# Sorting products of the dilated heads: exact bf16 parts and a bf16 0/1 matrix in place of float32

## The chip, the cores and the metric

One core of a Trainium2 chip runs the whole program. The time is the device time of one execution in microseconds (us); the figure for a kernel is the median of its runs. Engines are named as in the profile: PE (TensorE matmuls), PEld (TensorE weight loads, which lie beside the matmuls), DVE (VectorE), ACT (ScalarE), POOL (GpSimd), SP (the queue that issues most transfers). L547 is line 547 of the kernel before.

## The reference

The reference is one encoder block on a 1024 x 1024 float32 input: RMSNorm, a combined q/k/v projection, two groups of attention heads (4 differential heads, 8 dilated heads), an output projection with a residual, then RMSNorm, a router, 16 expert-choice SwiGLU experts and a last RMSNorm. What matters here is the mix of patterns in the dilated heads. Each pattern gives an output and the logarithm of its softmax denominator, and the patterns are mixed by a softmax over those logarithms:

```python
lse = jax.nn.logsumexp(s, axis=-1)
p = jnp.exp(s - lse[..., None])
o = jnp.einsum('brhnqk,brhnkd->brhnqd', p.astype(v.dtype), vn)
...
w = jax.nn.softmax(jnp.stack(lses, axis=0), axis=0)
o = jnp.sum(w[..., None] * jnp.stack(outs, axis=0).astype(jnp.float32), axis=0)
```

The kernel does not form the logarithms. For each query it keeps a (negated) maximum and a sum of exponentials per branch, and computes the mixing weights from these.

## The kernel before

**Stages.** Up to about 55 us: the first norm, its transposes and the first projection block. From there to about 400 us the eight dilated heads run, two heads to a unit, four units, with the twelve projection blocks poured in between as filler for PE. From about 390 us to 640 us the four differential heads run, then the output projection, the second norm, the router and the ranking, and from about 740 us on the experts, whose weights stream from memory through a ring of tiles.

**One dilated unit.** It is cut into 8 groups (two heads by four parts `j`). For each group there are four steps: `scores` (eight matmuls into the tile `ps`, L154 through the helper `mm`; the biased maximum on DVE, L416; the exponential and its sum on ACT, L418), `turn` (eight transposes into two `pt` tiles, L157 through the helper `tp`, with copies on ACT and DVE), `mix` (ten matmuls into `av`) and `gather` (L537, L538). The loop over the groups runs these as a pipeline: at step n it emits `scores(n)`, filler, one late step of the unit before if there is one, `turn(n-1)`, filler, `mix(n-2)`, `gather(n-2)`, filler.

**The two statistics tiles.** The near branch keeps its maxima and sums in `stN`, in natural order of the queries. The other branch works on queries sorted by their position modulo 4, so its maxima and sums, in `stM`, are in that order: each is a tile of 128 partitions by 32 float32 (two heads, maximum and sum, eight tiles of queries). Both get the maximum from DVE (L416) and the sum from ACT (L418).

**The late steps.** After the last `gather` of a unit four late steps are queued, one of them emitted in each later group, and for the fourth unit all at once: `regroup`, then `weights` and `spread`, then `combine(0)` and `combine(1)`. `regroup` (L541 to L551) brings `stM` into natural order by multiplying with 0/1 matrices, which are 128-column cuts of the tile `sort`: 16 float32 calls of 8 columns, which the profile shows as 32 matmuls and 32 weight loads, into a `pt` tile of the pool `ps_t` (two buffers, shared with the transposes), and one DVE copy to `sM`:

```python
for c in range(4):
    for r in range(4):
        x = 128 * c - r + 3
        nc.tensor.matmul(pm[:, :, c], sort[:, x:x + 128],
                         U["stM"].rearrange("p i s (r a) -> p r a i s", r=4)[:, r],
```

`weights` (L557 to L567) forms the mixing weights on DVE and ACT, `spread` (L574) widens them on POOL into `wr`, `combine` transposes `wr` on PE, mixes on DVE (L586 to L589), splits the result (L96) and stores it to `o_d` through SP (L592). The matrix `sort` is made once: an iota on POOL (L734) and a compare on DVE (L735).

**What sets the order.** PE, DVE, ACT, POOL and SP each run their instructions in a fixed order. That order is made when the program is built, by a scheduler that goes by program order, by what is ready and by its own estimate of durations: an instruction that is ready early may be put on an idle engine far ahead of its place in the program.

**What follows the dilated heads.** `open_left` frees their tiles, and the loads of the first differential head (L617, L618 for q and k, L621 for the bias, L627 for v) are issued on SP, some of them behind the stores of the last unit (L592).

Of the kernel before, what the change touches and what calls it, by code (L numbers as in the profile page):

```python
# [10 lines left out]
F32 = mybir.dt.float32  # L11
F32R = mybir.dt.float32r
BF = mybir.dt.bfloat16
I32 = mybir.dt.int32
AF = mybir.ActivationFunctionType
OP = mybir.AluOpType
# [3 lines left out]
S = 1024  # L20
D = 1024
NT = S // 128
# [60 lines left out]
def tile_hybrid_encoder_block(ctx, tc, x, norm1_g, w_in, lam_v, subln_g, w_out, rel_bias, hot,  # L83
                              norm2_g, w_router, w_moe, norm_f_g, steps, out, n_experts=E, dbg=None):
    nc = tc.nc
# [108 lines left out]
    ps_t = st_p.enter_context(tc.tile_pool(name="ps_t", bufs=2, space=PS))  # L194
# [231 lines left out]
    def dilated_unit(u):  # L426


        U = {}
# [110 lines left out]

        def regroup():  # L541

            pm = ps_t.tile([128, 2, 4, 2, 2], F32, name="pt")
            for c in range(4):
                for r in range(4):
                    x = 128 * c - r + 3
                    nc.tensor.matmul(pm[:, :, c], sort[:, x:x + 128],  # L547
                                     U["stM"].rearrange("p i s (r a) -> p r a i s", r=4)[:, r],
                                     start=(r == 0), stop=(r == 3))
            U["sM"] = sm_a.tile([128, 2, 2, NT], F32, name="sM")  # L550
            nc.vector.tensor_copy(U["sM"].rearrange("p i s (a c) -> p a c i s", a=2), pm)  # L551

        def weights():
            stN, sM = U["stN"], U["sM"]
# [22 lines left out]
        def combine(n):  # L577
# [3 lines left out]
            for k in range(2):  # L581
                pr = ps_t.tile([128, 4, 128], F32, name="pt")
                for t in range(4):
# [11 lines left out]
                   lambda i=i, j=j: gather(i, j)) for i in range(2) for j in range(4)]  # L595
        loads = [lambda i=i, h=h: load(i, h) for i in range(2) for h in range(2)]
        return loads, groups, [regroup, lambda: (weights(), spread(0), spread(1)), lambda: combine(0), lambda: combine(1)]

    def dense_unit(u):
# [114 lines left out]
    PA = {}  # L714
    fill = projections()

    def run(gen, n):
        for _ in range(n):
            next(gen, None)
# [10 lines left out]
            nc.gpsimd.memset(r32(tl), 0.0)  # L730
        PA["pair"].append(pr)

    sort = PA["dw"].tile([128, 516], F32, name="sort", bufs=1)
    nc.gpsimd.iota(sort.bitcast(I32), pattern=[[1, 516]], base=-3, channel_multiplier=-4)  # L734
    nc.vector.tensor_scalar(sort, sort.bitcast(I32), 0.0, None, op0=OP.is_equal)  # L735
    run(fill, FILL1)

    loads, groups = [], []
# [200 lines left out]
    with st_w as st:  # L939
# [4 lines left out]
        ps_t = st.enter_context(tc.tile_pool(name="ps_t3", bufs=2, space=PS))  # L944
# [290 lines left out]
    rem = rt.tile([128, NT, E], F32, name="tok")  # L1235
# [337 lines left out]
```

## Time and profile before

| what | value |
|---|---|
| median of 3 runs | 2278.7 us (2278.2 to 2278.9) |
| the profiled execution | 2276.6 us, its span 2274.8 us |
| PE busy | 2180.2 us, 96% of the span |
| DVE busy | 1891.9 us, 83% |
| ACT busy | 1601.4 us, 70% |
| POOL busy | 218.3 us, 10% |
| mean granted clock of PE | 0.981 |
| chain that ended last | PE 86%, DVE 5%, DMA 4%, issue 2%, ACT 2% |

The profile is of one execution. Its span runs from the first to the last instruction; the execution's time has about 1.8 us more, which lies around the span. Busy times overlap between engines, so what a change in one stage is worth is read from that stage: from its timeline, from what each engine waited for there, and from the chain of waits that ended last. In the windows view the clock is that which was granted to TensorE, as a share of full speed.

### The profile page before, as it was taken

Reading aid. Unit: us, or ns where it says so; the run is one execution under the profiler, and the core shown is the slowest. Engines: PE = TensorE matmul, PEld = TensorE weight load, DVE = VectorE, ACT = ScalarE, POOL = GpSimd, SP = SyncE. Lnnn points to the kernel's source line nnn. Section 1 sums busy time; section 2 is a strip of 40 time slices with the busy share of each in tenths; the row PEclk is TensorE's granted clock in tenths of the full one; section 3 lists DMA queues with packets and bytes.
Section 4 is the critical chain, followed back from the end, with each engine's and each line's share of the span. In section 5 each row is a group of like instructions: output and inputs, shape, how many; then the busy total and the mean of one; then the engine's idle time right before and its main releaser. Section 6 shows DMA issues by size and latency. Waiting matters only on the chain.

```text
span 2274.8 us, 31909 instructions
## 1 busy us (share of the span) xinstructions
PE 2180.2 (96%) x11115; PEld 1619.0 (71%) x11235; DVE 1891.9 (83%) x2870; ACT 1601.4 (70%) x2431; POOL 218.3 (10%) x244
## 2 busy tenths in 40 slices
PE   8999999889996999999999999999999999999995
PEld 7899989667874566666766766676676676666663
DVE  6466674567777999999899999999999999999996
ACT  5576773456753567777787777787777777877785
POOL 1000100245533000000000000000000000000000
PEclk9999999999997999999999999999999999999997
DMA  5866555579568899999999999999999999999983
GB/s 182 236 177 196 173 156 154 167 189 246 183 195 284 278 352 391 368 391 388 375 390 373 387 381 373 404 373 383 383 378 401 365 384 390 374 387 380 387 347 130
DMA packets 172750, 708.26 MB, mean 311 GB/s; under 512 B 19690, under 2 KB 54634, under 8 KB 106658
## 3 DMA queue, kind: packets, MB, share of 16 engines
q1 hardware_dynamic: 160452, 670.46, 79.8%
q0 software_dynamic: 7184, 25.69, 3.9%
q10 hardware_dynamic: 4952, 10.05, 1.2%
q8 instruction: 89, 1.46, 0.3%
q14 instruction: 73, 0.60, 0.1%
HBM read 649.89 MB, written 57.75 MB: 311 GB/s over the span
## 4 chain that ended last, share of the span: by engine, by line
PE 86%; DVE 5%; DMA 4%; issue 2%; ACT 2%; POOL 0%; SPq 0%; ACTq 0%; POOLq 0%; DVEq 0%
PE pg L1343 14%; PE pg L1344 14%; PE pg L1352 13%; PE pm L154 10%; PE py L1385 7%; PE py L1384 7%; PE py L1381 6%; PE av L154 4%; PE pt L157 3%; PE ps L154 3%; PE py L154 2%; PE px L1364 2%; DVE wl L1315 1%; DMA w<-in_w_moe_dram 1%; PE pt L547 1%
## 5 line engine op out<-in xcount | busy, mean ns | idle before, releaser
L1315 DVE TENSOR_TENSOR wl<-w,wh 128x1024 bf16<-128x1024 f32 (+1 forms) x1062 | 1236.3, 1213 | 75.4 <-ACT wh L1313 72.0
L1313 ACT ACTIVATE wh<-w 128x1024 fp32r<-128x1024 f32 (+1 forms) x1070 | 1041.6, 1041 | 8.6 <-DMA h_d<-xp 5.7
L1343 PE MATMUL pg<-wh,xh 128*128 128x512 f32 x1408 | 569.2, 404 | 0.0
L1344 PE MATMUL pg<-wh,xl 128*128 128x512 f32 x1408 | 552.4, 392 | 1.4 <-DVE xl L96 1.4
L1352 PE MATMUL pg<-wl,xh 128*128 128x512 bf16 x1313 | 316.5, 380 | 6.3
L1384 PE MATMUL py<-wh,eh 128*128 128x512 f32 x704 | 310.7, 441 | 0.0
L1343 PEld LDWEIGHTS pg<-wh,xh 128*128 128x128 f32 x1408 | 264.7, 188 | 56.3 <-issue 2.0
L1344 PEld LDWEIGHTS pg<-wh,xl 128*128 128x128 f32 x1408 | 265.1, 188 | 53.8 <-DVE xl L96 2.2
L1385 PE MATMUL py<-wh,el 128*128 128x512 f32 x704 | 278.3, 395 | 0.0
L1352 PEld LDWEIGHTS <-xh 128*128 128x128 bf16 x1408 | 123.6, 98 | 170.0 <-issue 45.1
L1370 ACT ACTIVATE eh<-px 128x256 fp32r<-128x256 f32 x176 | 67.6, 384 | 166.1 <-PE px L1364 166.1
L1381 PE MATMUL py<-wl,eh 128*128 128x512 bf16 x701 | 180.4, 379 | 1.0 <-ACT eh L1370 0.9
L1384 PEld LDWEIGHTS py<-wh,eh 128*128 128x128 f32 x704 | 132.4, 188 | 44.3
L1357 ACT ACTIVATE sg<-pg 128x256 f32<-128x256 f32 x176 | 67.5, 384 | 135.6 <-PE pg L1352 135.6
L1385 PEld LDWEIGHTS py<-wh,el 128*128 128x128 f32 x704 | 132.5, 188 | 28.7 <-issue 0.4
L154 PE MATMUL pm<-hT,wh 128*128 128x512 f32 x464 | 147.7, 399 | 0.1
L1381 PEld LDWEIGHTS <-eh 128*128 128x128 bf16 x704 | 68.8, 98 | 80.4 <-ACT eh L1370 1.2
L1444 POOL DMA_INDIRECT x_d<-row,idx x15 | 24.1, 1607 | 933.8 <-ACT row L1443 933.8
L154 PE MATMUL pm<-wh,hT 128*128 128x256 f32 x512 | 102.6, 291 | 0.4 <-ACT hT L96 0.2
L154 PEld LDWEIGHTS pm<-hT,wh 128*128 128x128 f32 x464 | 85.0, 190 | 16.0 <-DVE ee L361 0.5
L96 DVE TENSOR_TENSOR pl<-pt,ph 128x512 fp32r<-128x512 f32 x96 | 65.2, 683 | 36.2 <-ACT ph L96 36.2
L418 ACT ACTIVATE e<-e,nm 128x1024 f32<-128x1024 f32 x64 | 73.4, 1147 | 27.5 <-DVE nm L416 21.1
(299 smaller groups left out, 2907.4 us busy)
## 6 DMA issues: line engine op xcount, KB each, us to landing
w<-in_w_moe_dram SPq DMA_DIRECT2D x514, 1024.0 KB, 7.3
w<-in_w_moe_dram SPq DMA_DIRECT2D x56, 256.0 KB, 4.3
wraw<-in_w_in_dram SPq DMA_DIRECT2D x48, 256.0 KB, 3.7
v_d<-ee SPq DMA_DIRECT2D x16, 512.0 KB, 3.7
q_d<-ee SPq DMA_DIRECT2D x16, 512.0 KB, 3.7
k_d<-ee SPq DMA_DIRECT2D x16, 512.0 KB, 3.5
k<-k_d SPq DMA_DIRECT2D x16, 512.0 KB, 6.5
xt<-in_x_dram SPq DMA_DIRECT2D x8, 512.0 KB, 6.8
```

Source lines behind the costliest of these rows:

```text
L154: return pin(nc.tensor.matmul(*args, **kw))
L157: return pin(nc.tensor.transpose(*args, **kw))
L418: nc.scalar.activation(e, e, AF.Exp, bias=nm, scale=-1.0, accum_out=l)
L1313: hi = nc.scalar.activation(wh[:, cs], src, AF.Copy)
L1315: sub = eng.tensor_sub(wl[:, cs], src, r32(wh)[:, cs])
L1343: hh = nc.tensor.matmul(pg, xh[:, k, :], wh, start=(k == 0), stop=False)
L1344: mm_ = nc.tensor.matmul(pg, xl[:, k, :], wh, start=False, stop=False)
L1352: low = nc.tensor.matmul(pg, top(xh)[:, k, :], cut(k)[1], start=False, stop=(k == KD - 1))
L1370: in_turn(nc.scalar.activation(eh, pt, AF.Copy))
L1381: low.append(lambda j=j, c=c, ns=ns, n=n: nc.tensor.matmul(py[:, ns], top(eh)[:, j, :], wl(c, 512), start=(s == 0 and j == 0), stop=False))
L1384: nc.tensor.matmul(py[:, ns], eh[:, j, :], wh(c, 512), start=False, stop=False),
L1385: nc.tensor.matmul(py[:, ns], el[:, j, :], wh(c, 512), start=False, stop=(s == NS - 1 and j == 1))))
```

## The change

The matrix `sort` becomes bf16. `regroup` first cuts `stM` into three bf16 parts whose sum is the float32 value (24 bits in three times 8), with five instructions on POOL: a copy to bf16, a subtraction, a copy, a subtraction, a copy. The 16 calls then multiply bf16 by bf16 with 24 columns each instead of 8, into a `pt` tile three times as large, and two DVE reductions add the three parts, in place of the one copy. The integer scratch for making `sort` is taken from a tile of the pool `er`, since `sort` itself is too narrow now.

```diff
         def regroup():
-            pm = ps_t.tile([128, 2, 4, 2, 2], F32, name="pt")
+            st, rem = U["stM"], PA["dw"].tile([128, 2, 2, NT], F32, name="rem", bufs=1)
+            parts = PA["dw"].tile([128, 2, 2, NT, 3], BF, name="parts", bufs=1)
+            for n in range(3):
+                nc.gpsimd.tensor_copy(parts[:, :, :, :, n], st)
+                if n < 2:
+                    nc.gpsimd.tensor_sub(rem, st, parts[:, :, :, :, n])
+                    st = rem
+            pm = ps_t.tile([128, 2, 4, 2, 2, 3], F32, name="pt")
             for c in range(4):
                 for r in range(4):
                     x = 128 * c - r + 3
                     nc.tensor.matmul(pm[:, :, c], sort[:, x:x + 128],
-                                     U["stM"].rearrange("p i s (r a) -> p r a i s", r=4)[:, r],
+                                     parts.rearrange("p i s (r a) n -> p r a i s n", r=4)[:, r],
                                      start=(r == 0), stop=(r == 3))
             U["sM"] = sm_a.tile([128, 2, 2, NT], F32, name="sM")
-            nc.vector.tensor_copy(U["sM"].rearrange("p i s (a c) -> p a c i s", a=2), pm)
+            for i in range(2):
+                nc.vector.tensor_reduce(U["sM"][:, i].rearrange("p s (a c) -> p a c s", a=2), pm[:, :, :, i],
+                                        axis=mybir.AxisListType.X, op=OP.add)
...
-    sort = PA["dw"].tile([128, 516], F32, name="sort", bufs=1)
-    nc.gpsimd.iota(sort.bitcast(I32), pattern=[[1, 516]], base=-3, channel_multiplier=-4)
-    nc.vector.tensor_scalar(sort, sort.bitcast(I32), 0.0, None, op0=OP.is_equal)
+    sort = PA["dw"].tile([128, 516], BF, name="sort", bufs=1)
+    places = PA["er"].tile([128, S], F32, name="ed").bitcast(I32)[:, 0:516]
+    nc.gpsimd.iota(places, pattern=[[1, 516]], base=-3, channel_multiplier=-4)
+    nc.vector.tensor_scalar(sort, places, 0.0, None, op0=OP.is_equal)
```

## Rows read from the trace of the kernel before

**Rows 1.** Windows view: busy us (count) of each engine, PEclk, DMA share, GB/s.

```profile
90.00:400.00 310.00, 307.96 (x2100) 282.55 (x2098) 193.91 (x557) 200.24 (x497) 18.69 (x57) 0.99 0.62 174
860.00:2100.00 1240.00, 1234.66 (x5694) 859.09 (x5773) 1141.24 (x1251) 968.08 (x1223) 38.21 (x27) 1.00 0.98 383
```

**Rows 2.** Chain that ended last, 60 to 420 us: start, us, what.

```profile
164.10 3.47 PE pt L547 x32
...
236.82 3.67 PE pt L547 x32
...
304.29 3.47 PE pt L547 x32
...
370.54 3.47 PE pt L547 x32
...
388.47 10.90 DMA w<-q_d
```

**Rows 3.** Timeline, first regroup: start, us, engine, what, [idle before <-releaser].

```profile
163.93 3.63 PE L547 MATMUL pt<-stM,sort 128*128 128x8 f32 x32
...
167.42 0.63 PE L157 MATMUL pt<-ident,ed 128*128 128x128 f32 x4
...
167.60 0.21 DVE L551 COPY sM<-pt 128x32 f32<-128x32 f32 x1 [1.55 <-PE pt L547]
```

**Rows 4.** Timeline, PE at 810 us: 16-column bf16 products, then 112 to 16 columns.

```profile
810.86 0.36 PE L1193 MATMUL px<-gt,ones_b 128*128 128x16 bf16 x8 [1.30 <-DVE gt L1190]
...
811.18 0.38 PE L1182 MATMUL pr<-eq,ones_b 128*128 128x112 bf16 x7
```

**Rows 5.** One line's view, L1193: ns min/median/max, first and last start.

```profile
L1193 PEld LDWEIGHTS <-ones_b x8: 95/96/99, 810.9 to 811.0; 128*128 128x128 bf16 x8
```

**Rows 6.** Windows view around the second and fourth regroup, columns as in Rows 1.

```profile
236.70:240.40 3.70, 3.70 (x35) 3.66 (x33) 1.88 (x3) 2.43 (x4) 0.00 (x0) 1.00 0.55 164
240.40:243.40 3.00, 3.00 (x17) 3.00 (x17) 1.16 (x3) 1.86 (x3) 0.00 (x0) 0.58 0.77 291
243.40:247.00 3.60, 3.60 (x29) 3.60 (x28) 2.81 (x12) 3.49 (x11) 0.16 (x1) 0.88 0.09 35
...
307.60:311.00 3.40, 3.40 (x21) 2.91 (x21) 2.02 (x7) 1.31 (x3) 0.16 (x1) 1.00 0.02 5
...
374.00:377.40 3.40, 3.40 (x10) 2.62 (x10) 1.60 (x10) 0.23 (x1) 1.25 (x3) 0.50 1.05 223
```

**Rows 7.** Timeline after the second regroup, ACT and the PE weight loads.

```profile
241.54 0.60 ACT L512 ACTIVATE pair<-pt 128x512 fp32r<-128x512 f32 x1 [2.36 <-PE pt L157]
...
254.77 0.19 PEld L154 LDWEIGHTS pm<-hT,wl 128*128 128x128 f32 x1 [0.45 <-DVE wl L334]
```

**Rows 8.** Tile view of stM: ns min/median/max, first and last start.

```profile
L418 ACT ACTIVATION_READ_ACCUMULATOR ed<-ed,stM x64: 185/188/202, 91.1 to 353.8; 128x1 f32 x64
```

**Rows 9.** Timeline of POOL: start, us, what, [idle before <-releaser].

```profile
1.18 0.12 POOL L952 MEMSET rank<- 128x40 f32 x1
...
16.02 0.45 POOL L292 TENSOR_TENSOR rl<-rb,rh 34x128 fp32r<-34x128 f32 x1
...
141.01 0.21 POOL L447 MEMSET k<- 128x128 f32 x1 [7.18 <-PE ps L154]
...
376.15 2.28 POOL L574 COPY wr<-ea 128x512 f32<-128x512 f32 x4 [32.67 <-DVE ea L567]
```

**Rows 10.** Tile view of wr: ns min/median/max, first and last start.

```profile
L574 POOL COPY wr<-ea x16: 604/613/3033, 175.4 to 377.8; 128x512 f32<-128x512 f32 x16
```

**Rows 11.** Timeline at 2096 us, a DVE reduction from PSUM.

```profile
2096.45 0.16 DVE L1223 TENSOR_REDUCE num<-pr 128x1 f32<-128x2 f32 x1 [1.74 <-PE pr L1221]
```

**Rows 12.** Timeline, way from the last unit to the differential heads.

```profile
383.87 2.50 SPq L592 DMA_DIRECT2D o_d<-wr  x2
...
386.42 0.56 SPq L621 DMA_DIRECT2D w<-ta_d  x1
...
397.88 1.09 PE L154 MATMUL ps<-w 128*128 128x512 f32 x4
...
402.15 2.04 PE L154 MATMUL ps<-w 128*128 128x512 f32 x4 [3.18 <-issue]
```

## The prediction

> **What bounds the kernel now.** I read the windows first, then the chain of waits, then the timeline around the four regroups. From 90 to 400 us PE is busy for 308 of 310 us, while DVE and ACT are at 63% and 65% and POOL at 6% [rows 1]: in the stage of the change PE is the bound, and there is always a projection block to fill it. The chain that ended last agrees: all four regroups stand on it, with 3.47, 3.67, 3.47 and 3.47 us, together 14.08 us [rows 2]. The timeline shows why it is so much. A regroup writes only 8 columns per product, yet its 32 float32 products hold PE from 163.93 until the next transposes at 167.42 us, 3.49 us or 109 ns each [rows 3]. The time goes into weights that are loaded anew for each product.
>
> What comes later doesn't undo a shift. The experts' stage has PE busy for 99.6% and the DMA engines at 98% [rows 1], and whichever of the two sets its pace, it starts when the stages ahead of it let it: its loads hang on tiles that these free, not on the clock on the wall. So a microsecond taken from PE before 370 us should be a microsecond at the end.
>
> **The change part by part.** *The products.* 32 float32 products per unit become 16 of bf16, each in one pass, with 24 columns. The nearest rows are eight bf16 products of 16 columns, each with its own load: 0.36 us for all eight, where one alone takes 0.17 [rows 4, 5], so they follow each other at (0.36 - 0.17) / 7 = 27 ns. Seven of 112 down to 16 columns take 0.38 us [rows 4], 35 ns apart, so that 24 columns instead of 16 cost next to nothing. At 31 ns, 16 products are 0.5 us. Per unit 14.08 / 4 - 0.5 = 3.0 us is saved, and 12.1 us over four. The bounds are 27 ns (0.43 us, 12.4 us saved) and the 109 ns of today's products (1.74 us, 7.1 us saved); I take the bf16 rows, since they have type and shape of the new ones. One thing differs: half of the cuts of the matrix start at an odd bf16 column.
>
> A load of 128 columns is one place where the notes speak against the change: the Trainium skill, "TensorE: Matmul & The Clock Gate", section "LDWEIGHTS (loading the stationary operand)", gives a load as its columns over 1.2 GHz whatever they hold, 107 ns here, and 16 in a row would then be 1.7 us (an estimate from that page). The row shows loads of 95 to 99 ns each, of which eight start within about 0.2 us [rows 5], so they overlap. I go by the row, and keep the other as a rival.
>
> *The clock.* After the second and the fourth regroup the granted clock fell: 0.58 from 240.4 to 243.4 us and 0.88 until 247.0, and 0.50 from 374.0 to 377.4; after the third it stayed at 1.00 [rows 6]. What PE did before it fell was over 3.5 us of 8-column products at full clock [rows 6]. Lost were 0.42 x 3.0 + 0.12 x 3.6 = 1.7 us and 0.5 x 3.4 = 1.7 us of PE's time. With 0.5 us of products I expect neither fall, but I count nothing for it. In unit 2 ACT is the next in line: it stood idle for 2.36 us until the transposes behind the regroup came, and at 254.77 us PE was already waiting for weights that ACT and DVE had to cut [rows 7]. If ACT sets the pace, this unit gains 2.4 us, if PE does, 3.1 + 1.7 = 4.8; I take 3.1, nearer to ACT's row. In unit 4 PE has too little work anyway: it finishes its scores at about 399 us and starts the next at 402.15, after a load that took 10.90 us [rows 2, 12]. PE work done faster there only lengthens that wait.
>
> *The fourth unit's own path.* The loads that PE waits for at 402 us stand on SP behind the two stores of the last unit [rows 12], and these behind weights, spread and combine. All of that starts where the regroup ends, so the 3.0 us of this unit count through this path. It gets two reductions for the one copy of 0.21 us [rows 3]. The nearest reduction took 0.16 us on 2 elements [rows 11]; between 0.16 and 0.3 us each I take 0.2, hence 0.2 us more. In units 1 to 3 the later maxima wait for nothing but combine, whose PE work is filler; nothing.
>
> *The split on POOL.* Five instructions on 32 elements each: the rows bound one by 0.12 us (a memset of 40 elements) and 0.45 us (a subtraction of 128) [rows 9], at worst by 3.03 us, the longest of the 512-element copies, whose median is 0.61 [rows 10]. I take 0.25 each, 1.3 us per unit. I cost it at nothing, because it is covered: unit 1 ends its scores at 141.0 us, when POOL's memset of a key tile is released [rows 9], and some 4 us later its sums are there; the regroup comes at 163.9 [rows 3]. In unit 4 the last sum is written at 354.0 [rows 8], the regroup starts 16 us later, and POOL is idle for 32.67 us until 376.15 [rows 9]. That the scheduler uses such room is to be seen from a memset of the ranking, which ran at 1.18 us [rows 9], hundreds of microseconds ahead of its place. What is queued on POOL behind the split (memsets of keys, values and scores) has several microseconds of slack each. If this cover is gone, PE's queue waits for the split with all that stands behind it; that is a rival. Making the matrix keeps its iota and its compare, now from a borrowed buffer that is free then: nothing.
>
> **The sum.** 12.1 - 0.2 = 11.9 us less. The profiled execution took 2276.6 us and would take 2264.7; the median of the runs is 2.1 us above it, and 2278.7 - 11.9 = 2266.8 us.
>
> **The rivals.** *Loads one after the other.* If the weight loads of the odd cuts, or all, don't overlap, 16 x 98 ns [rows 5] are 1.6 us per unit, and (3.5 - 1.6) x 4 - 0.2 = 7.4 us are saved: 2271.3 us. For it: today's products stand at 109 ns. Against it: the bf16 rows.
>
> *The gain is taken in by the next wait.* ACT in unit 2 and the loads at 402 us show such waits already. If DMA throughput and not the end of the stores sets the landing at 399 us (the DMA share was 1.05 from 374.0 to 377.4 [rows 6]), all that the four units gain meets the same landing, and if the same holds for the experts' weights at a share of 0.98 [rows 1], between 0 and 4 us are left, 2276.7 us in the middle. Against it: every one of these transfers is issued by something that moves forward too.
>
> *PE waits for the split (slower).* The place is PE's queue at the first product of each unit. If the scheduler leaves the split beside the regroup, the whole of it stands on the path; it costs as much as is saved at five instructions of 0.6 us, the median of the 512-element copies. At 0.8 us it is 4.0 - 3.0 = 1.0 us per unit lost, 4 us in all, and PE standing still would lower the clock in units 1 and 3 as well, 2 x 1.7 us: 2286.1 us. The Trainium skill, "GPSIMD Engine Reference", section "Engine selection", sends elementwise work to VectorE, as GpSimd is about twice as slow with two inputs; that matters only if the split is uncovered, and no row here shows these five. Against this rival: 19 and 16 us of cover.
>
> **How the numbers follow.** The forecast has 0.67, loads one after the other 0.10, the gain taken in 0.11, PE waiting for the split 0.07; 0.05 is for an order that the scheduler makes anew with other waits, split evenly over the three results. Single steps at this length are uncertain by one fall of the clock, 1.7 us, either way. The forecast's own range is 2263 (12.4 - 0.2 and both falls of 1.7 us won) to 2270; taking in the rival of the loads and one more fall of the clock, and 2 us below for a luckier order, the range is 2261 to 2273. A measurement of this kernel can tell about 0.2%, 4.6 us, from no change. Forecast and loads give faster, with a third of the rest, 0.79; the gain taken in gives the same time, 0.12; the split on the path slower, 0.09.
>
> **What would show it.** The 16 products within 0.6 us per unit, at about 30 ns; the five POOL instructions ending microseconds before; no idle of PE that ends with them; the granted clock at 1.00 after all four; the dense scores of 402.15 us at about 390. It is wrong if the products stand at 100 ns, if PE waits for POOL ahead of the first of them, or if the dense scores come 12 us sooner and the end doesn't.

## The result and the profile after

The change made the kernel faster by 0.5%, little but clear of the noise: 2268.2 us median (2264.1 to 2271.0, six runs) against 2279.9 us (2278.2 to 2285.0, six runs) on the same chip, a ratio of 0.995 with a 95% interval of 0.9936 to 0.9964, 11.6 us. The forecast was 2266.8 us, 11.9 less. The profiled execution took 2268.57 us, span 2266.8, clock 0.981 as before; its partner took 2276.63, faster than any of the six runs of before. So the two traces differ by 8.1 us only, and 8.1 is what they can explain. PE's busy time over the span fell by 12.0 us, from 2180.2 to 2168.2.

The timeline of PE after the change; columns as in [rows 3]:

```profile
163.90 0.57 PE L555 MATMUL pt<-parts,sort 128*128 128x24 bf16 x16
164.32 0.42 PE L157 MATMUL pt<-ident,ed 128*128 128x128 f32 x2
...
233.60 0.57 PE L555 MATMUL pt<-parts,sort 128*128 128x24 bf16 x16
234.02 0.36 PE L154 MATMUL pm<-wh,hT 128*128 128x256 f32 x1
...
235.61 0.50 PE L154 MATMUL ps<-kc,qc 128*128 128x256 f32 x2 [0.55 <-ACT kc L422]
...
247.88 0.50 PE L154 MATMUL pm<-hT,wl 128*128 128x512 f32 x1 [0.40 <-DVE wl L334]
...
298.12 0.56 PE L555 MATMUL pt<-parts,sort 128*128 128x24 bf16 x16
...
361.27 0.57 PE L555 MATMUL pt<-parts,sort 128*128 128x24 bf16 x16
361.69 0.48 PE L154 MATMUL pm<-hT,wh 128*128 128x512 f32 x1
```

Sixteen products hold PE from 163.90 to 164.32, 0.42 us or 26 ns each, where 32 held it for 3.49 [rows 3]; the other units give 0.42, 0.41 and 0.42. No idle time stands in brackets at any of the four, so PE waited for nothing there. It does wait behind the second, for ACT's `kc` at 235.61 and for DVE's `wl` at 247.88: work that PE used to cover [rows 7] now ends last. The view of line L555 (ns min/median/max, first and last start):

```profile
L555 PEld LDWEIGHTS <-sort x64: 95/97/101, 163.9 to 361.6; 128*128 128x128 bf16 x64
L555 PE MATMUL pt<-parts,sort x64: 176/181/191, 163.9 to 361.7; 128*128 128x24 bf16 x64
```

A load takes 97 ns (96 in [rows 5]), and a product 181, but they start 26 ns apart: they overlap, odd cuts and even ones alike. In before a load of the float32 kind took 192 ns, and these pairs followed each other at 109 ns:

```profile
L547 PEld LDWEIGHTS pt<-stM,sort x128: 186/192/193, 163.8 to 373.7; 128*128 128x128 f32 x128
```

Why a float32 pair takes four times the spacing of a bf16 pair, no run separates. The timeline of POOL shows the split, three of its five instructions in the first unit and two in the fourth:

```profile
144.82 0.24 POOL L547 CAST parts<-stM 128x32 bf16<-128x32 f32 x1 [2.52 <-ACT ed L418]
145.15 0.25 POOL L549 TENSOR_TENSOR rem<-stM,parts 128x32 f32<-128x32 f32 x1
...
146.09 0.24 POOL L547 CAST parts<-rem 128x32 bf16<-128x32 f32 x1
...
344.98 0.24 POOL L547 CAST parts<-stM 128x32 bf16<-128x32 f32 x1 [10.61 <-ACT ed L418]
...
346.25 0.24 POOL L547 CAST parts<-rem 128x32 bf16<-128x32 f32 x1
```

The split runs from 144.82 to 146.33, 1.5 us, and is done 17.6 us before PE needs it; in the fourth unit 14.8 us before. The view of the tile `sM` has the two reductions (0.20 us each):

```profile
L560 DVE TENSOR_REDUCE sM<-pt x8: 199/203/209, 165.9 to 362.0; 128x16 f32<-128x48 f32 x8
```

The windows of the stage and of the 3.4 us from each regroup on, with the columns of [rows 1]:

```profile
90.00:400.00 310.00, 300.83 (x2053) 271.19 (x2052) 199.11 (x573) 203.58 (x505) 23.94 (x78) 0.98 0.64 181
...
163.60:167.00 3.40, 3.40 (x36) 2.90 (x36) 3.09 (x16) 3.12 (x9) 0.00 (x0) 1.00 0.96 279
233.40:236.80 3.40, 2.85 (x36) 2.48 (x35) 2.32 (x6) 3.35 (x6) 0.00 (x0) 1.00 0.50 137
298.00:301.40 3.40, 3.40 (x36) 2.95 (x35) 2.35 (x14) 3.09 (x10) 0.16 (x1) 1.00 0.49 178
361.00:364.40 3.40, 3.40 (x30) 2.58 (x29) 1.71 (x11) 0.23 (x1) 0.31 (x1) 1.00 1.05 328
```

The clock stays at 1.00 behind all four, where it fell to 0.58 and 0.50 before [rows 6]. What the fourth unit leads to is seen first in the timeline of SP's queue:

```profile
370.64 2.49 SPq L602 DMA_DIRECT2D o_d<-wr  x2
373.19 0.56 SPq L631 DMA_DIRECT2D w<-ta_d  x1
```

and then in the chain that ended last (start, us, what):

```profile
375.23 13.50 DMA w<-q_d
388.73 2.62 issue
391.35 2.06 PE ps L154 x4
```

The stores left at 370.64 and the bias load behind them at 373.19, 13.2 us sooner than at 383.87 and 386.42 [rows 12]; but a load on the chain took 13.50 us, not 10.90 [rows 2], and the third dense scores came at 391.35 instead of 402.15, 10.8 us sooner.

**Where the 8.1 us come from.** The timelines have fixed marks: the first product of each regroup, the issue of the bias load, the third dense scores, the experts' first product (L1343 before, L1354 after: 741.09 and 730.46) and the end of the span. The time from mark to mark, in us, each the difference of two starts:

```
                                before   after   difference
start to regroup 1              163.93  163.90   -0.03
regroup 1 to regroup 2           72.82   69.70   -3.12
regroup 2 to regroup 3           67.38   64.52   -2.86
regroup 3 to regroup 4           66.24   63.15   -3.09
regroup 4 to bias load           16.05   11.92   -4.13
bias load to 3rd dense scores    15.73   18.16   +2.43
to the experts' first product   338.94  339.11   +0.17
to the end of the span         1533.76 1536.33   +2.57
sum                            2274.85 2266.79   -8.06
```

The four units won 13.2 us. Of these 2.4 went into the loads and 2.6 at the start of the experts. For the latter the windows of before:

```profile
740.00:744.00 4.00, 2.56 (x9) 1.59 (x8) 4.00 (x8) 1.20 (x2) 0.00 (x0) 0.67 0.60 184
744.00:748.00 4.00, 4.00 (x20) 2.85 (x20) 2.58 (x5) 1.06 (x1) 0.00 (x0) 1.00 0.88 303
```

and of after:

```profile
728.00:732.00 4.00, 3.04 (x10) 2.07 (x10) 4.00 (x5) 1.19 (x2) 1.16 (x1) 0.50 0.37 108
732.00:736.00 4.00, 3.02 (x8) 2.43 (x9) 1.58 (x5) 1.06 (x1) 0.00 (x0) 0.50 0.91 308
736.00:740.00 4.00, 4.00 (x13) 2.80 (x13) 2.17 (x4) 0.00 (x0) 0.00 (x0) 0.61 0.44 139
740.00:744.00 4.00, 3.95 (x21) 2.56 (x21) 1.83 (x4) 1.62 (x4) 0.00 (x0) 1.00 0.02 4
```

PE comes to the experts' first product after a stretch with little work, at half clock in both. If the clock rose in one step, a mean of 0.67 from 740 to 744 puts it at 742.6 us, 1.6 behind that product; after, 0.61 from 736 to 740 puts it at 739.1, 8.7 behind it. This seems to go with the execution and not with the change: over the thirteen traces told of here the last interval lies between 1532.6 and 1536.5 us, and float32 products are found near both ends (1533.8 in before and e2, 1536.1 in e10).

### The profile page after: what moved, and what is told of

The parts are those of the page before. It is cut to its first block, busy times and chain, and to the rows that moved or that the text cites. A ratio compares the mean times of both kernels' runs of the same rounds, so it can differ in the third digit from the quotient of the medians.

```text
span 2266.8 us, 31806 instructions
## 1 busy us (share of the span) xinstructions
PE 2168.2 (96%) x11051; PEld 1604.7 (71%) x11171; DVE 1891.6 (83%) x2874; ACT 1600.3 (71%) x2431; POOL 223.6 (10%) x264
## 4 chain that ended last, share of the span: by engine, by line
PE 84%; DVE 6%; DMA 5%; issue 2%; ACT 2%; SPq 0%; POOL 0%; POOLq 0%; ACTq 0%; DVEq 0%
PE pg L1354 14%; PE pg L1355 14%; PE pg L1363 13%; PE pm L154 10%; PE py L1396 7%; PE py L1395 7%; PE py L1392 6%; PE av L154 4%; PE ps L154 3%; PE pt L157 3%; PE px L1375 2%; PE py L154 1%; DVE wl L1326 1%; DMA xt<-xa_d 1%; DMA w<-q_d 1%
## 5 line engine op out<-in xcount | busy, mean ns | idle before, releaser
L1354 PE MATMUL pg<-wh,xh 128*128 128x512 f32 x1408 | 570.7, 405 | 0.0
L1354 PEld LDWEIGHTS pg<-wh,xh 128*128 128x128 f32 x1408 | 265.5, 189 | 56.5 <-issue 2.1
```

The costliest lines, as they stand in the source:

```text
L1354: hh = nc.tensor.matmul(pg, xh[:, k, :], wh, start=(k == 0), stop=False)
```

## The experiments

The theory: the time is won by the PE time of the products, the split is covered, and the fourth unit's share counts through its stores and the loads behind them. The rivals: it is the clock and not the products; the split costs; the gain of some unit is taken in by the next wait.

### One part of the units alone: e1 and e2

In e1 units 1 to 3 have the new regroup and unit 4 the old one; in e2 it is the other way round (`u < 7`). The dense scores that the expectations of e1 to e4 call the second are those called the third here. The matrix stays float32, and the bf16 products read the upper halves of its elements.

```diff
         def regroup():
+            if u == 7:
+                pm = ps_t.tile([128, 2, 4, 2, 2], F32, name="pt")
...
+                nc.vector.tensor_copy(U["sM"].rearrange("p i s (a c) -> p a c i s", a=2), pm)
+                return
```

> Units 1 to 3 keep the bf16 products, unit 4 has the float32 products of before (the bf16 matrix is read as the upper halves of the float32 one). Theory (each regroup gives back PE's time, the fourth is partly taken in by the loads behind it): unit 1 to 3 gain 3.1, 2.8 and 3.2 us as in the changed kernel, the second dense scores (402.15 us before, 391.35 after) start at about 393.0, 9.1 us before 402.15, and the clock falls to 0.5 after the fourth regroup; the whole is about 9 us faster than before. Rival (unit 4's path through stores and loads is worth its full 3 us, and what is missing was lost elsewhere): 394.2 us or later. Rival (the clock, not the PE time, is the gain): 400 us.

> Only unit 4 has the bf16 products, units 1 to 3 the float32 products of before. Theory: stores of the last unit are issued about 4 us earlier than before (3.0 of products, the rest from the clock that no longer falls behind them), but the load that PE waits for lands only about 1.6 us earlier, so the second dense scores start at about 400.5 us; the whole is 1 to 2 us faster than before, within what can be measured. Rival (the path from the regroup through the stores sets the landing): scores at 398 to 399 us, 3 to 4 us faster. Rival (the loads alone set it): 402 us, no gain.

Measured: e1 2270.4 us against 2277.8 for before, ratio 0.9969 (0.9956 to 0.9983); e2 2278.0 us, ratio 1.000 (0.9987 to 1.0013). The whole of e2 says little, as its ten runs lie between 2272.5 and 2282.1. By the medians the two parts are worth 7.4 us and nothing, less together than the 11.6 of the change; with intervals of 3.9 to 10.0 us and of 3.0 us either way they can't settle whether the parts add up. The marks say more (us):

```
                       before    e1     e2   after  after again (e5)
regroup 1 to 2          72.82  69.79  74.40  69.70  69.76
regroup 2 to 3          67.38  64.67  66.84  64.52  64.67
regroup 3 to 4          66.24  63.19  67.83  63.15  63.18
regroup 4 to bias load  16.05  16.06  11.91  11.92  11.91
to 3rd dense scores     15.73  16.27  16.11  18.16  16.01
```

Each unit with bf16 products gives the time of after within 0.2 us, each with float32 that of before within 1.6: up to the bias load the shares are separate and add up. The third dense scores stood at 392.57 us in e1 and at 400.55 in e2, within 0.5 us of what was expected. Unit 4 is worth 4.1 us up to the bias load in both pairs. What comes of it at the dense scores hangs on the loads, which take 15.7 to 18.2 us on this stretch, and 16.01 and 18.16 in two executions of the very same kernel. That kernel, run again on another chip beside e6 to e8:

> The changed kernel again, for a second profile and more times. Theory (about 10 us are gained by 400 us; what the loads before the dense scores take, 18.2 us from the issue of the bias load to the second dense scores against 15.7 before, and where the clock rises after the ranking, vary from run to run): units 1 to 3 gain the same 3.1, 2.8 and 3.2 us to 0.2 us, the loads take anything from 15.7 to 19 us, and the median lies 9 to 13 us below before. Rival (both belong to the changed order): 18.2 us again, and again 2.4 us lost at the start of the experts.

Measured: 2266.0 us against 2278.9, ratio 0.9953 (0.9937 to 0.997), so the result stands.

e2 also prices the clock. It fell behind its first and third regroup, and not behind its second:

```profile
166.90:170.30 3.40, 3.40 (x17) 2.81 (x16) 1.53 (x6) 0.60 (x1) 0.00 (x0) 0.66 0.20 74
241.40:244.80 3.40, 3.40 (x31) 3.40 (x31) 2.34 (x11) 2.39 (x3) 0.16 (x1) 1.00 0.83 313
308.30:311.70 3.40, 3.40 (x14) 2.83 (x14) 1.54 (x6) 0.60 (x1) 0.00 (x0) 0.55 0.02 5
```

The same float32 interval is 74.40 instead of 72.82 us and 67.83 instead of 66.24 with a fall, 1.6 us each; in the second unit, where before had the fall, it is 67.38 instead of 66.84, only 0.5. e10 below is a float32 kernel whose clock fell behind the second and the third regroup; its intervals, 72.75, 67.36 and 67.79 us, repeat this to 0.1.

### The cover taken from the split: e4

POOL's first copy waits for the newest score or mixing product on PE, so that it can't run ahead.

```diff
-                nc.gpsimd.tensor_copy(parts[:, :, :, :, n], st)
+                cut = nc.gpsimd.tensor_copy(parts[:, :, :, :, n], st)
+                if n == 0:
+                    wait_for(cut, newest[0])
```

> The changed kernel with the first of the five POOL instructions waiting for the newest matmul of scores or mix that stands ahead of the regroup, so that the split no longer runs some 17 us ahead but at the regroup. Theory (the split costs nothing since it is covered): uncovered it takes about 1.6 us and two hand-overs, 2 us; PE has projection products to put in between, so the products move behind some of them and the second dense scores come 0 to 2 us later than 391.35 us, the whole 0 to 2 us slower than the changed kernel. Rival (PE's queue stands still for the split in each unit): 2 us of idle PE per unit, and the clock falls in some: 6 to 10 us slower than the changed kernel, near the time of before.

The timeline of POOL in e4, first and last instruction of the first unit's split:

```profile
164.32 0.24 POOL L549 CAST parts<-stM 128x32 bf16<-128x32 f32 x1 [3.54 <-PE ps L154]
...
165.59 0.24 POOL L549 CAST parts<-rem 128x32 bf16<-128x32 f32 x1
```

and that of PE:

```profile
164.68 0.39 PE L154 MATMUL pm<-hT,wh 128*128 128x512 f32 x1
165.88 0.56 PE L559 MATMUL pt<-parts,sort 128*128 128x24 bf16 x16 [0.81 <-POOL parts L549]
```

Now PE does wait, 0.81 us here and 2.5 us in three such waits; for the rest it had been given filler. The fourth regroup stood at 362.87 us, 1.6 later than in after, and the third dense scores at 393.69, 2.3 later. The whole took 2268.5 us, ratio 0.9961 (0.9946 to 0.9975), which can't be told from after's 0.995. So the cover is worth 1.6 us up to the fourth regroup in this pair of traces, too little for the whole to show, and the clock stayed at 1.00 behind all four regroups: the wait that was feared is short.

### Products or clock: e6, e7

e6 computes the same product eight times over (128 products of the new kind per unit):

```diff
-            for c in range(4):
+            for c in range(32):
+                c = c % 4
```

> The changed kernel with the 16 bf16 products of each unit run eight times over (128 of them, each pass overwriting the one before). Theory (PE's time is what counts): 128 at 26 ns are 3.3 us per unit, about what the float32 products took, so the gains of units 1 to 3 vanish and the whole comes back to within 3 us of before; and since PE again does only narrow products for 3 us, the granted clock falls to about 0.5 after some of the four. Rival (it is the float32 kind and its loads, not the time): the gain stays, 9 us or more faster than before, and the clock stays at 1.00.

The timeline of PE in e6, first unit:

```profile
163.08 3.37 PE L556 MATMUL pt<-parts,sort 128*128 128x24 bf16 x128
166.29 0.64 PE L157 MATMUL pt<-ident,ed 128*128 128x128 f32 x4
```

The windows behind the first and the second regroup in e6:

```profile
166.20:169.60 3.40, 3.40 (x29) 2.92 (x26) 2.69 (x11) 2.40 (x7) 0.16 (x1) 1.00 0.36 128
240.30:243.70 3.40, 3.40 (x37) 3.40 (x34) 2.03 (x8) 3.38 (x12) 0.16 (x1) 1.00 0.57 215
```

The timeline of SP's queue in e6:

```profile
369.69 0.60 SPq L632 DMA_DIRECT2D w<-ta_d  x1
380.46 2.49 SPq L603 DMA_DIRECT2D o_d<-wr  x2
```

The products take 3.21 us, 25 ns each, where float32 took 3.49 (in the second unit they stand in two pieces, of 53 and 75, with scores between), and the intervals between the regroups are 72.55, 66.66 and 66.00 us, where before had 72.82, 67.38 and 66.24. In units 1 and 3, in which the clock didn't fall in either kernel, the interval is shorter by 0.27 and 0.24 us, what the products are shorter by. So in these two units it is PE's time that counts, and nothing else of the change does. The whole came out otherwise, and against what was expected: 2267.1 us, ratio 0.995 (0.9932 to 0.9968), as fast as after. The bias load stood at 369.69, ahead of the stores at 380.46, where it stood behind them before [rows 12]; DVE, which had waited for it at the first dense scores, 6.8 us in before and 9.6 in after, did not wait for it here; and the third dense scores came at 395.18 us, 7.0 sooner than before, with PE not waiting. So this time was won at the passage to the dense heads, where SP has another order. That order alone is not shown to be worth 11.8 us: e10 below puts all these loads ahead of the stores in the kernel before and wins 3.8, and the profiled execution of e6, the slowest of its eight runs, ends 4.3 us ahead of that of before. Where the rest of the medians' difference comes from stays open.

e7 keeps the float32 products and puts filler among them. One step of filler, about 2.8 us, stands between the first 16 and the last 16 products of a unit:

```diff
                     nc.tensor.matmul(pm[:, :, c], sort[:, x:x + 128],
...
+                if c == 1:
+                    run(fill, 1)
```

> The kernel before, its float32 regroup cut in two by half a projection group (1.4 to 2.7 us of wide products) between the second and the third quarter. PE's work is the same as before. Theory (the clock falls behind long stretches of narrow products, and this is worth little here, since ACT sets unit 2 and the loads set unit 4): the clock stays at 1.00 after all four, and the whole is within 2 us of before. Rival (the falls of the clock carried part of the gain): 3 us faster than before or more.

Measured: 2269.5 us against 2278.9, ratio 0.9962 (0.9948 to 0.9977), 9.4 us faster than before, though its products are float32; within 2 us had been expected. The clock was 1.00 behind all four regroups. The fourth regroup stood at 375.93 us and the third dense scores at 405.93, later than before, which says little, since a step of filler more stands in each unit, which PE then need not do behind them. But again the bias load went ahead of the stores, at 379.29 against 391.02, and PE did not run dry at the dense scores: from 400 to 410 us it was busy for 8.68 us at a clock of 1.00, where in before it was for 6.53 us at a mean of 0.56. The rival, that the falls of the clock behind the regroups carried part of the gain, is not refuted: they too are absent here, and e7 doesn't separate the two. Two experiments that were meant for the products had pointed to something else: what stands ahead of the dense loads on SP.

In or behind an unbroken run of float32 products the clock fell in 9 of 16 units (before 2 of 4, e1 1 of 1, e2 2 of 3, e8 and e10 2 of 4 each), with filler among them in none of 4, and behind bf16 products in none of 32. In 28 of these 32 the products took 0.4 us only; the test of the kind against the time are e6's four, of which three were unbroken, and at 9 in 16 three units without a fall come by chance about once in twelve. So that the kind decides, and not the length of the run, is not shown.

### The stores in front of the loads: e9, e10

The waits of SP from 355 to 400 us (us in total, times, longest), in before:

```profile
SPq L592 <- DVE wr L96: 13.4, 2, 11.7
```

and in after:

```profile
SPq L602 <- DVE wr L96: 9.4, 2, 7.8
```

SP waits up to 11.7 and 7.8 us for the last split of `wr`, with the dense loads behind it, and the DMA engines have little to do meanwhile. Windows of before:

```profile
378.00:382.00 4.00, 3.84 (x25) 2.93 (x24) 3.23 (x5) 0.88 (x2) 0.43 (x1) 1.00 0.13 30
382.00:386.00 4.00, 4.00 (x19) 3.34 (x18) 3.10 (x5) 0.98 (x2) 0.00 (x0) 1.00 0.31 118
386.00:402.00 16.00, 12.97 (x57) 10.34 (x56) 4.40 (x9) 4.35 (x9) 0.00 (x0) 0.98 0.99 221
```

A share of 0.13 and 0.31, and then 0.99 for 16 us while PE runs dry. So the two stores of the last unit were moved to POOL's queue, in e9 from after, in e10 from before:

```diff
-            nc.sync.dma_start(o_d[u].rearrange("h p s -> p h s")[:, :, ns], r32(wr))
+            (nc.gpsimd if u == 7 else nc.sync).dma_start(o_d[u].rearrange("h p s -> p h s")[:, :, ns], r32(wr))
```

> The changed kernel with one thing different: the two stores of the last dilated unit are issued by POOL, which is idle there, and not by SP. The order of every other instruction is the same. Theory (on SP the five loads of the first differential head stand behind these stores, which wait 7.8 us for DVE; the loads then take 16 to 18 us at a full DMA share, and PE waits for them): the bias load is issued at about 363.5 instead of 373.2 us, lands by 382, PE finds it there when it gets to the third dense scores, which start at 386 to 387 us instead of 391.35; with the clock not falling in that wait the whole is 4 to 7 us faster than the changed kernel, near 2261 us. Rival (DMA throughput alone sets the landing, or the loads need the memory of what the stores read): third dense scores at 390 us or later, whole within 2 us of the changed kernel.

> The same on the kernel before: float32 products, the two stores of the last unit on POOL. Theory (the queue behind the stores and the products are separate matters): the third dense scores start at about 399 us instead of 402.15 and the whole is 3 to 7 us faster than before, near 2273 us. The change of the products would then be worth about 9 to 12 us on top (against the run before this one). Rival (the gain of the products was mostly a matter of how the loads fell): this kernel is within 3 us of the changed kernel, 2266 to 2269 us.

Measured on one chip: e9 2260.7 us, ratio 0.9931 (0.9917 to 0.9945); e10 2273.2 us, ratio 0.9986 (0.9976 to 0.9996); before 2277.0. Both came out nearly as the theory had it. In e9 the bias load goes out at 362.35, 8.1 us ahead of the first store, and the third dense scores start at 385.73 (391.35 in after); in e10 they start at 398.52 (402.15 in before):

```profile
362.35 0.60 SPq L631 DMA_DIRECT2D w<-ta_d  x1
...
370.45 0.93 POOL L602 DMA_DIRECT2D o_d<-wr  x1 [4.81 <-DVE onm L599]
...
385.73 1.17 PE L154 MATMUL ps<-w 128*128 128x512 f32 x4 [0.98 <-DMA w<-k_d]
```

The windows of after over the dense scores:

```profile
380.00:390.00 10.00, 5.76 (x25) 4.12 (x23) 3.70 (x8) 3.75 (x8) 0.00 (x0) 0.88 1.04 196
390.00:400.00 10.00, 7.08 (x18) 4.71 (x19) 5.41 (x12) 4.29 (x8) 0.18 (x1) 0.61 0.46 162
```

and those of e9:

```profile
380.00:390.00 10.00, 7.70 (x32) 5.46 (x31) 5.51 (x11) 4.99 (x11) 0.00 (x0) 1.00 0.89 315
390.00:400.00 10.00, 7.88 (x34) 5.57 (x33) 8.57 (x19) 6.03 (x11) 5.48 (x5) 1.00 0.28 105
```

In after PE is busy for 5.76 of 10 us and then gets a mean of 0.61 of its clock; in e9 7.70 and 1.00. The two stores cost after 6.9 us in this pair of traces: its instructions on ACT, matched one by one with those of e9, stand 0.7 us later until 375 us and 7.6 us later from 400 on. By the ratios to before, 0.9931 against 0.995 and 0.9953, it is 4 to 5 us of the whole, from runs on different chips and with intervals that overlap a little, and 3.8 us for the float32 kernel (2277.0 - 2273.2; 0.9 to 5.5 by the interval). And e9 against e10 is the cleanest measure of the change itself, since the stores are out of the loads' way in both: 2273.2 - 2260.7 = 12.5 us; their traces differ by 13.0.

### The regroup emitted earlier: e3, e8, e11

If the fourth unit's path sets the landing of the loads, its late steps should start sooner. Regroup, weights and spread are queued at once when the unit's last scores are emitted, two groups earlier; combine stays. In e3 from after, in e8 from before, in e11 together with the stores on POOL:

```diff
-        return loads, groups, [regroup, lambda: (weights(), spread(0), spread(1)), lambda: combine(0), lambda: combine(1)]
+        return loads, groups, [regroup, lambda: (weights(), spread(0), spread(1))], [lambda: combine(0), lambda: combine(1)]
...
+        if n < N:
+            late += groups[n][2]
```

> The changed kernel with regroup, weights and spread queued two groups earlier (behind the scores of the unit's last group instead of behind its last gather), so that in unit 4 only combine, stores and loads follow the last gather. Theory (DMA throughput sets when the loads of the dense stage land): the stores of unit 4 are issued 2 to 4 us earlier and the second dense scores start less than 1 us earlier than in the changed kernel; the whole within 1.5 us of it. Rival (the end of the stores sets it): scores and end 2 to 4 us earlier.

> The kernel before (float32 products) with regroup, weights and spread queued two groups earlier, as in the run before it with bf16. Theory (earlier stores of the last unit and the new order are worth about 10 us by themselves, independent of the type of the products): 8 to 12 us faster than before, near 2267 us. Rival (the earlier place pays only with short products): within 4 us of before.

> The kernel with regroup, weights and spread two groups earlier (2257.4 us), and the two stores of the last unit on POOL too. Theory: there SP waits 4.5 us with the stores and the bias load goes out at 368.2 us; sent at once, the third dense scores move from 384.9 to about 383 us at most, since PE has to get there first, so 0 to 3 us are won: 2254 to 2257 us. Rival (the two edits do the same thing): no difference, 2257 us.

Measured: e3 2257.4 us (2253.4 to 2259.5) against 2277.8, ratio 0.9912 (0.9892 to 0.9933), the lowest median here, though its interval overlaps that of e9. Both the theory of e3 (within 1.5 us of after) and its rival (2 to 4 us) were too low. e8 2276.4 against 2278.9, ratio 0.9991 (0.9972 to 1.001): the same edit is worth nothing that could be measured with float32 products, where 8 to 12 us had been expected. e11 2261.3, ratio 0.9934 (0.9919 to 0.9949): no better than e9 without the edit, and 4 us above both values expected. The marks:

```
                  after     e3     e9    e11     e8
regroup 4        361.27 347.54 360.53 348.69 361.94
last stores      370.64 365.02 370.45 366.75 385.58
bias load        373.19 368.15 362.35 362.36 388.71
3rd dense scores 391.35 384.94 385.73 384.20 405.94
```

In e3 the stores leave 5.6 us sooner, the dense scores come 6.4 us sooner, and PE waits for 1.75 us instead of 4.85 and keeps its clock:

```profile
384.94 1.18 PE L154 MATMUL ps<-w 128*128 128x512 f32 x4 [1.75 <-issue]
```

e3 and e9 are thus two ways to much the same gain, loads that land about when PE gets to them (it still waits for 1.75 and 0.98 us). In e11 PE doesn't wait there at all, and the third dense scores come only 0.7 us sooner than in e3: the two don't add up. In e8 the stores left at 385.58, no sooner than before, though its regroup stood 8 us earlier: the scheduler made another order, whose first three intervals sum to 211.8 us instead of 206.4. Its clock also fell in the first and the fourth regroup, to 0.50 from 152.6 to 159.2 and from 364.2 to 370.8 us. Why the order is another stays open. e3 wins another 6 us over after behind the start of these scores (6.4 us there, 12.1 in the span). Part of that is the clock, since after has a mean of 0.61 from 390 to 400 us, at most 4 us of PE's time, where e3 has 1.00; the rest is not settled.

## Why the prediction was right

*The products.* Predicted 0.5 us per unit at 31 ns, measured 0.42 at 26 ns: 12.4 us saved on PE where 12.1 were written down. The row of eight bf16 products [rows 4, 5] was the right one to price by. The Trainium skill, "TensorE: Matmul & The Clock Gate", section "LDWEIGHTS (loading the stationary operand)", gives a load as its columns over 1.2 GHz, 107 ns for 128; the trace has 97 ns, so the duration is near it, but loads in a row follow each other at 26 ns, and the sum must not be made from their duration. The rival of loads one after the other is refuted, and the odd cuts cost nothing. "The time goes into weights that are loaded anew for each product" can be said of the float32 kind at most: each of e6's 128 bf16 products loads its own weights too, and they stand 25 ns apart.

*The split and the reductions.* Five instructions of 0.24 to 0.25 us, as estimated, covered by 17.6 us in unit 1 and 14.8 in unit 4; 0.20 us for a reduction, as estimated. e4 shows that the slower rival was priced too high as well: it had 4.0 us per unit on the path and two more falls of the clock, but PE bridges most of a late split with filler, and three waits came to 2.5 us with no fall at all.

*The clock.* That no fall would come was right. Counting nothing for it was about right in unit 2, where a fall costs only 0.5 us (e2) and ACT is the next in line, as the prediction had it from [rows 7]: without a fall on either side unit 2 gains 66.84 - 64.52 = 2.3 us, the 2.4 of ACT's row, and with it 2.86 against the 3.1 taken. In unit 4 it was not: up to the bias load 4.1 us were won, not 3.0 - 0.2, probably because the fall at 374 us [rows 6] slowed not only PE's filler but also the transposes on which the stores hang: both float32 fourth units of the table (before, e1) had a fall, and where there was none, in e10, regroup to first store took 12.90 us, 2.98 more than the 9.92 of e9. The step "PE work done faster there only lengthens that wait" overlooked these.

*The gain taken in.* As a rival it gave 2 us left of 12, and that was wrong; but it happened in part. In the profiled pair 2.4 us of unit 4's share went into longer loads and 2.6 into the clock at the experts' start. Neither belongs to the change: the loads took 16.0 us in e5, and the experts' stage varies by 3.9 us whatever the products are. Medians (11.6, 12.9 in e5) and e9 against e10 (12.5) agree with the predicted 11.9 better than the one pair of traces. How near the number came is partly luck: the interval of the first ratio is 8.2 to 14.6 us, and the 1.3 us that unit 4 won beyond its term (4.1 against 2.8) had no place in the sum.

## What to carry to other kernels

Price a run of narrow matmuls by the spacing of a like run in the trace, not by the duration of one load or one product; here an exact split into three bf16 parts was worth it though the product itself is tiny. Divide the trace by marks that both kernels have, and compare the intervals: four of them showed the gain to 0.2 us where single executions of the whole differed by several. And look at what a queue waits for in front of the loads of the next stage: moving two stores off SP was worth, by the medians, about another third of what the change itself gave.

## What was not expected

A store that waits at the head of SP's queue holds back the loads behind it, and that costs twice: in before the DMA engines stood at a share of 0.13 to 0.31 for 8 us, and in after PE was idle for 4.85 us and then ran at a mean of 0.61 of its clock for 10. Two stores moved to POOL's queue gave 4 to 5 us in after, 3.8 in before. And the fall of the clock at the regroups may go with the kind of products and not only with the time that narrow products hold PE: unbroken float32 products of 8 columns, 3.5 us at full clock, had a fall in or behind them in 9 of 16 units, 3.2 us of bf16 products of 24 columns (e6) in none of 4, and the float32 ones with filler among them in none of 4. Four units each are too few to show it.
